# Log-softmax backward: two rows per partition, and all transfers on GpSimd's queue

## The chip, the core and the metric

The kernel runs on one core of a Trainium2 chip. Such a core has engines that work side by side[...]: TensorE (PE, unused here), VectorE (DVE), ScalarE (ACT), GpSimd (POOL) and SyncE (SP). Sixteen transfer engines move data between the large memory of the chip (HBM) and the core's SBUF, a memory of 128 partitions. A transfer (DMA) is issued by an engine's queue, here SP's before and POOL's after, and is split over the sixteen transfer engines. The metric is the device time of one execution in microseconds (us), and less is better. Each kernel is executed several times; one execution is recorded by the profiler.

## What is computed

```python
batch, seq_len, vocab = 8, 1024, 8192          # y and dy: float32

def reference(y, dy):
    softmax_x = np.exp(y)
    sum_dy = np.sum(dy, axis=-1, keepdims=True)
    return (dy - softmax_x * sum_dy).astype(np.float32)
```

There are 8 x 1024 = 8192 rows of 8192 numbers. Each row of dy is summed, and each element of the result takes one exponential, one product and one sum. Two arrays of 268.4 MB are read and one is written, 805.3 MB in all.

## The kernel before

The rows are cut into 64 tiles of 128 rows, one row to each partition, so a tile has 128 x 8192 numbers, 4 MiB, and a partition holds one run of 32 KiB of it.

For each tile, line 65 loads dy into `dy_t`, line 67 loads y into `y_t`, and line 69 lets VectorE sum the row of `dy_t` and put the negative sum in `s_t`. The helper `subtract_scaled_exp` then goes through the tile in four pieces of 2048 columns: ScalarE writes exp(y) to a tile `e_t` in PSUM, a second small memory next to the engines (line 19), and VectorE computes e_t * s_t + dy_t in one scalar_tensor_tensor and writes it over `dy_t` (line 20). Line 75 stores `dy_t`.

Tiles come in batches of three, after a first batch of one. Inside a batch the tiles are loaded and computed one after the other; the stores of the batch stand behind all of them. SP issues all 192 transfers, in the order of the program. An issue that has to wait holds back everything behind it in its queue: a load waits until its buffer is free, and a store until VectorE has finished its tile. The buffers are four `dy_t` (BATCH + 1), two `y_t`, and two `e_t` in PSUM[...]. The order within an engine is the order of the program; semaphores between the engines are put in by the framework.

```python
64            dy_t = dyp.tile([P, D], fp32, name="dy_t")
65            nc.sync.dma_start(out=dy_t[:], in_=dy_f[sl])
66            y_t = yp.tile([P, D], fp32, name="y_t")
67            nc.sync.dma_start(out=y_t[:], in_=y_f[sl])
...
72            subtract_scaled_exp(nc, psum, y_t, dy_t, s_t[:], CD)
73            done.append((sl, dy_t))
74        for sl, dy_t in done:
75            nc.sync.dma_start(out=out_f[sl], in_=dy_t[:])
```

Of the kernel before, what the change touches and what calls it, by code (L numbers as in the profile page):

```python
# [1 line left out]

# [5 lines left out]


ACT_EXP = mybir.ActivationFunctionType.Exp  # L10
ALU = mybir.AluOpType


def subtract_scaled_exp(nc, psum, y_part, dy_part, neg_sum, width):

    total = y_part.shape[-1]
    for c in range(0, total, width):
        e_t = psum.tile([128, width], mybir.dt.float32, name="e_t")
        nc.scalar.activation(e_t[:], y_part[:, c : c + width], ACT_EXP)  # L19
        nc.vector.scalar_tensor_tensor(  # L20
            out=dy_part[:, c : c + width],
            in0=e_t[:],
            scalar=neg_sum,
            in1=dy_part[:, c : c + width],
            op0=ALU.mult,
            op1=ALU.add,
        )


@with_exitstack  # L30
def kernel(
    ctx: ExitStack,
    tc: tile.TileContext,
    y: bass.AP,
    dy: bass.AP,
    out: bass.AP,
):


    nc = tc.nc  # L40
    P = nc.NUM_PARTITIONS
    fp32 = mybir.dt.float32

    y_f = y.flatten_outer_dims()
    dy_f = dy.flatten_outer_dims()
    out_f = out.flatten_outer_dims()
    N, D = y_f.shape
    n_tiles = N // P
    assert N == n_tiles * P
    CD = 2048  # L50
    BATCH = 3

    dyp = ctx.enter_context(tc.tile_pool(name="dyp", bufs=BATCH + 1))
    yp = ctx.enter_context(tc.tile_pool(name="yp", bufs=2))
    psum = ctx.enter_context(tc.tile_pool(name="psum", bufs=2, space=bass.MemoryType.PSUM))
    stats = ctx.enter_context(tc.tile_pool(name="stats", bufs=8))

    first = n_tiles % BATCH
    starts = [0] * bool(first) + list(range(first, n_tiles, BATCH))
    for b, e in zip(starts, starts[1:] + [n_tiles]):  # L60
        done = []
        for i in range(b, e):
            sl = ts(i, P)
            dy_t = dyp.tile([P, D], fp32, name="dy_t")
            nc.sync.dma_start(out=dy_t[:], in_=dy_f[sl])  # L65
            y_t = yp.tile([P, D], fp32, name="y_t")
            nc.sync.dma_start(out=y_t[:], in_=y_f[sl])  # L67
            s_t = stats.tile([P, 1], fp32, name="s_t")
            nc.vector.tensor_reduce(  # L69
                out=s_t[:], in_=dy_t[:], axis=mybir.AxisListType.X, op=ALU.add, negate=True  # L70
            )
            subtract_scaled_exp(nc, psum, y_t, dy_t, s_t[:], CD)
            done.append((sl, dy_t))
        for sl, dy_t in done:
            nc.sync.dma_start(out=out_f[sl], in_=dy_t[:])  # L75


# [1 line left out]
_INS = ['y', 'dy']  # L79
_OUTS = [((8, 1024, 8192), 'float32')]  # L80


# [23 lines left out]
```

## Time and profile before

| | |
|---|---|
| median of 4 runs | 1871.87 us (1871.59 to 1871.94) |
| the profiled execution, its own time | 1871.79 us |
| its span in the profile | 1869.8 us |
| bytes moved in it | 805.38 MB, 431 GB/s on average |
| sum of a row tile (line 69) | 64 times, 8680 ns each |
| exponential of a piece (line 19) | 256 times, 1877 ns each |
| multiply and add of a piece (line 20) | 256 times, 2344 ns each |
| transfers | 64 of dy, 64 of y, 64 of out, 4 MiB each |

The span runs from the first to the last recorded event on the core; the time of an execution is about 2 us longer. Engine rows name an engine, its busy time, its share of the span and its instructions. The rows of 40 digits cut the span into 40 equal slices; a digit is the busy share in tenths, 9 meaning 90% or more, and the row GB/s is what the transfer engines moved in each slice. "L20" is line 20 of the kernel, "SPq" the issuing of transfers by SP. An entry such as "ACT e_t L19 <- DMA y_t<-in_y_dram" says that ScalarE, before it could write e_t, waited for the load of y.

The trace also holds a record of each packet that a transfer engine moved, with its start, length and size, and of the semaphore updates with which transfers report that they have landed.

### The profile page before, as it was taken

The numbers are of one execution on the slowest core, as the hardware profiler recorded it, in microseconds if no ns is written. First come the engines' busy times: TensorE is split into PE (matmuls) and PEld (weight loads), VectorE is DVE, ScalarE is ACT, GpSimd is POOL, SyncE is SP. The second block draws the span as 40 slices with busy tenths as digits, with TensorE's granted clock in tenths as the row PEclk, the third lists the DMA queues.
The fourth block names the chain that finished last, engine by engine and source line by source line (L and its number), as shares of the span: only waits on it lengthen the run. The fifth ranks groups of instructions, "written<-read, shape, count | busy, mean of one in ns | idle before, by whom it ended". The sixth has DMA issues, their size and how long they took to land.

```text
span 1869.8 us, 1067 instructions
## 1 busy us (share of the span) xinstructions
DVE 1136.0 (61%) x320; ACT 477.5 (26%) x257; POOL 0.2 (0%) x4
## 2 busy tenths in 40 slices
DVE  6738384756657383839384655647383839374655
ACT  2214131313223131314131313213131414131322
POOL 0000000000000000000000000000000000000000
DMA  9999999999999999999999999999999999999998
GB/s 404 436 428 437 428 435 434 430 434 430 435 432 433 433 430 435 430 435 432 432 434 431 435 432 433 433 431 434 432 434 434 430 435 430 435 430 434 433 431 386
DMA packets 27656, 805.38 MB, mean 431 GB/s; under 512 B 3072, under 2 KB 3072, under 8 KB 3072
## 3 DMA queue, kind: packets, MB, share of 16 engines
q1 hardware_dynamic: 27648, 805.32, 100.0%
q14 instruction: 8, 0.07, 0.0%
HBM read 536.87 MB, written 268.44 MB: 431 GB/s over the span
## 4 chain that ended last, share of the span: by engine, by line
DMA 61%; DVE 13%; ACT 5%; SPq 1%; issue 0%; DVEq 0%; ACTq 0%
DMA y_t<-in_y_dram 61%; DVE dy_t L20 13%; ACT e_t L19 5%; SPq L65 0%; SPq L75 0%; DVEq L101 0%; ACTq L19 0%; SPq L67 0%
## 5 line engine op out<-in xcount | busy, mean ns | idle before, releaser
L69 DVE TENSOR_REDUCE s_t<-dy_t 128x1 f32<-128x8192 f32 x64 | 555.5, 8680 | 575.5 <-DMA dy_t<-in_dy_dram 575.5
L19 ACT ACTIVATE e_t<-y_t 128x2048 f32<-128x2048 f32 x256 | 476.2, 1877 | 1370.2 <-DMA y_t<-in_y_dram 1295.1
L20 DVE SCALAR_TENSOR_TENSOR dy_t<-e_t,s_t,dy_t 128x2048 f32<-128x2048 f32 x256 | 584.1, 2344 | 139.5 <-ACT e_t L19 139.5
L19 ACT ACT_TABLE_LOAD x1 | 1.3, 1283 | 0.7 <-PEq L90 0.7
L90 POOL MEMSET const-uint8-127<- 128x1 uint8 x1 | 0.1, 102 | 0.0
L90 POOL MEMSET const-bfloat16-1.0<- 128x1 bf16 x1 | 0.1, 101 | 0.0
L90 POOL MEMSET const-float32-0.0<- 128x1 f32 x1 | 0.1, 98 | 0.2 <-issue 0.2
L90 POOL MEMSET const-float32-1.0<- 128x1 f32 x1 | 0.1, 98 | 0.0
## 6 DMA issues: line engine op xcount, KB each, us to landing
dy_t<-in_dy_dram SPq DMA_DIRECT2D x64, 4096.0 KB, 45.4
y_t<-in_y_dram SPq DMA_DIRECT2D x64, 4096.0 KB, 36.4
out_dram<-dy_t SPq DMA_DIRECT2D x64, 4096.0 KB, 27.7
```

What stands on the lines that cost most here:

```text
L19: nc.scalar.activation(e_t[:], y_part[:, c : c + width], ACT_EXP)
L20: nc.vector.scalar_tensor_tensor(out=dy_part[:, c : c + width], in0=e_t[:], scalar=neg_sum, in1=dy_part[:, c : c + width], op0=ALU.mult, o ...
L69: nc.vector.tensor_reduce(out=s_t[:], in_=dy_t[:], axis=mybir.AxisListType.X, op=ALU.add, negate=True)
L90: nc = _bacc.Bacc("TRN2", target_bir_lowering=False, num_devices=1)
```

## The change

The rows are grouped by 256 instead of 128, and each partition holds two neighbouring rows (R = 2). dy is loaded, and out is stored, in transfers of 8 MiB with one run of 64 KiB per partition; y is loaded in two transfers of 4 MiB per group, one for each of the two rows of a partition, in runs of 32 KiB. There are 32 groups. One reduction per group sums both rows.

The exponential is written over `y_t` in SBUF, in pieces of 4096 columns, and PSUM is no longer used. The buffers are two `dy_t` of 64 KiB and two `y_t` of 32 KiB per partition.

The order of the queue is new as well: the load of the next group's dy is issued ahead of the store of this group, and both stand ahead of the next group's y. The store of the last group but one comes after the last loads, and the last store is split in two. All transfers are issued by GpSimd[...], instead of SP. POOL then has this sequence: dy(0), y(0) twice, dy(1), store(0), y(1) twice, dy(2), store(1), and so on; at the end y(31) twice, store(30), store(31) twice.

```diff
-    for c in range(0, total, width):
-        e_t = psum.tile([128, width], mybir.dt.float32, name="e_t")
-        nc.scalar.activation(e_t[:], y_part[:, c : c + width], ACT_EXP)
-        nc.vector.scalar_tensor_tensor(
-            out=dy_part[:, c : c + width],
-            in0=e_t[:],
-            scalar=neg_sum,
-            in1=dy_part[:, c : c + width],
-            op0=ALU.mult,
-            op1=ALU.add,
-        )
...
-    CD = 2048
-    BATCH = 3
+    R = 2
+    G = N // (P * R)
+    CD = D // 2
...
+    dy_v = dy.flatten_outer_dims().rearrange("(g p r) d -> g p (r d)", p=P, r=R)
...
-    dyp = ctx.enter_context(tc.tile_pool(name="dyp", bufs=BATCH + 1))
-    yp = ctx.enter_context(tc.tile_pool(name="yp", bufs=2))
-    psum = ctx.enter_context(tc.tile_pool(name="psum", bufs=2, space=bass.MemoryType.PSUM))
-    stats = ctx.enter_context(tc.tile_pool(name="stats", bufs=8))
+    dyp = ctx.enter_context(tc.tile_pool(name="dyp", bufs=2))
+    yp = ctx.enter_context(tc.tile_pool(name="yp", bufs=R))
+    stats = ctx.enter_context(tc.tile_pool(name="stats", bufs=2))
...
+    def load_dy(g):
+        dy_t = dyp.tile([P, R * D], fp32, name="dy_t")
+        nc.gpsimd.dma_start(out=dy_t[:], in_=dy_v[g])
+        s_t = stats.tile([P, R], fp32, name="s_t")
+        nc.vector.tensor_reduce(
+            out=s_t[:],
+            in_=dy_t[:].rearrange("p (r d) -> p r d", r=R),
+            axis=mybir.AxisListType.X,
+            op=ALU.add,
+            negate=True,
+        )
+        return dy_t, s_t
+
+    def load_y(g):
+        y_ts = []
+        for r in range(R):
+            y_t = yp.tile([P, D], fp32, name="y_t")
+            nc.gpsimd.dma_start(out=y_t[:], in_=y_v[g][:, r * D : (r + 1) * D])
+            y_ts.append(y_t)
+        return y_ts
+
+    def compute(dy_t, s_t, y_ts):
+        for r in range(R):
+            for c in range(0, D, CD):
+                e = y_ts[r][:, c : c + CD]
+                d = dy_t[:, r * D + c : r * D + c + CD]
+                nc.scalar.activation(e, e, EXP)
+                nc.vector.scalar_tensor_tensor(
+                    out=d, in0=e, scalar=s_t[:, r : r + 1], in1=d, op0=ALU.mult, op1=ALU.add
+                )
+
+    def store(g, dy_t, parts=1):
+        w = R * D // parts
+        for k in range(parts):
+            nc.gpsimd.dma_start(
+                out=out_v[g][:, k * w : (k + 1) * w], in_=dy_t[:, k * w : (k + 1) * w]
+            )
+
+    cur = load_dy(0)
+    for g in range(G):
+        if g < G - 1:
+            y_ts = load_y(g)
+            compute(*cur, y_ts)
+            nxt = load_dy(g + 1)
+            if g < G - 2:
+                store(g, cur[0])
+                cur = nxt
+            else:
+                held, cur = cur, nxt
+        else:
+            y_ts = load_y(g)
+            compute(*cur, y_ts)
+            store(g - 1, held[0])
+            store(g, cur[0], parts=R)
```

More of the change, by code (lines that the diff above doesn't have):

```diff
@@ L7 @@
 from concourse.bass import ts
-ACT_EXP = mybir.ActivationFunctionType.Exp
+EXP = mybir.ActivationFunctionType.Exp
 ALU = mybir.AluOpType
-def subtract_scaled_exp(nc, psum, y_part, dy_part, neg_sum, width):
-    total = y_part.shape[-1]
-    for c in range(0, total, width):
-        e_t = psum.tile([128, width], mybir.dt.float32, name="e_t")
-        nc.scalar.activation(e_t[:], y_part[:, c : c + width], ACT_EXP)
-        nc.vector.scalar_tensor_tensor(
-            out=dy_part[:, c : c + width],
-            in0=e_t[:],
-            scalar=neg_sum,
-            in1=dy_part[:, c : c + width],
-            op0=ALU.mult,
-            op1=ALU.add,
-        )
 @with_exitstack
@@ L42 @@
     fp32 = mybir.dt.float32
[L44 to L49, printed above, removed]
-    CD = 2048
-    BATCH = 3
-    dyp = ctx.enter_context(tc.tile_pool(name="dyp", bufs=BATCH + 1))
-    yp = ctx.enter_context(tc.tile_pool(name="yp", bufs=2))
-    psum = ctx.enter_context(tc.tile_pool(name="psum", bufs=2, space=bass.MemoryType.PSUM))
-    stats = ctx.enter_context(tc.tile_pool(name="stats", bufs=8))
@@ L58 @@
[L58 to L65, printed above, removed]
-            y_t = yp.tile([P, D], fp32, name="y_t")
[L67 to L70, printed above, removed]
-            )
[L72 to L75, printed above, removed]
+    N, D = y.flatten_outer_dims().shape
@@ new lines @@
+    R = 2
+    G = N // (P * R)
+    assert N == G * P * R
+    CD = D // 2
+    y_v = y.flatten_outer_dims().rearrange("(g p r) d -> g p (r d)", p=P, r=R)
+    dy_v = dy.flatten_outer_dims().rearrange("(g p r) d -> g p (r d)", p=P, r=R)
+    out_v = out.flatten_outer_dims().rearrange("(g p r) d -> g p (r d)", p=P, r=R)
+    dyp = ctx.enter_context(tc.tile_pool(name="dyp", bufs=2))
+    yp = ctx.enter_context(tc.tile_pool(name="yp", bufs=R))
+    stats = ctx.enter_context(tc.tile_pool(name="stats", bufs=2))
```

## The prediction, made before the changed kernel had run

> **What bounds the kernel now.** I read the page first: engine shares, then the slices.
>
> ```profile
> DVE 1136.0 (61%) x320; ACT 477.5 (26%) x257; POOL 0.2 (0%) x4
> ...
> DMA  9999999999999999999999999999999999999998
> GB/s 404 436 428 437 428 435 434 430 434 430 435 432 433 433 430 435 430 435 432 432 434 431 435 432 433 433 431 434 432 434 434 430 435 430 435 430 434 433 431 386
> DMA packets 27656, 805.38 MB, mean 431 GB/s; under 512 B 3072, under 2 KB 3072, under 8 KB 3072
> ...
> q1 hardware_dynamic: 27648, 805.32, 100.0%
> q14 instruction: 8, 0.07, 0.0%
> ```
>
> No engine computes more than 61% of the span, while the transfer engines are busy in every slice and move 428 to 437 GB/s from the second to the second-last. The chain of waits says "DMA 61%; DVE 13%; ACT 5%", which looks like compute on the path; it is not, since the data movers have queued work under all of it. The waits confirm that the compute engines wait for data:
>
> ```profile
> ACT e_t L19 <- DMA y_t<-in_y_dram: 1295.1, 63, 40.7
> DVE s_t L69 <- DMA dy_t<-in_dy_dram: 575.5, 22, 28.3
> ```
>
> (Columns: total us, times, longest.) Then stages, to see where rate is lost (us, DVE, ACT and POOL busy, clock, DMA share, GB/s):
>
> ```profile
> 0.00:46.00 46.00, 27.30 (x7) 11.54 (x7) 0.20 (x4) 1.00 0.97 405
> 400.00:487.40 87.40, 52.95 (x16) 22.32 (x12) 0.00 (x0) 1.00 1.00 433
> 1827.00:1870.00 43.00, 22.37 (x8) 9.32 (x5) 0.00 (x0) 1.00 0.88 380
> ```
>
> A batch of three tiles (9 transfers of 4 MiB) takes 87.4 us and has no hole. What is left is the rate inside the stream, some 3 us at the head and some 5 us at the tail.
>
> Last I read the trace's packet records. A 32 KiB data packet takes 1213 ns (median), the next starts 3 to 4 ns before its end, and each transfer ends on each of the 16 engines with a 4-byte completion packet of 9 ns. The first engine to complete does so at 1835.32, 1845.00, 1854.68 and 1864.36 us for the last four transfers: 9.684 us each. The last engine completes the first transfer at 12.46 against 12.11 for the first engine, the last transfer at 1868.55 against 1864.36. So the slowest engine falls 3.8 us behind the fastest over the run, and it sets the end. The eight 8 KiB instruction fetches (row q14) come at 271, 359, 438, 930, 1106, 1164, 1542 and 1844 us; completions of one engine each drop back by 0.5 to 1.0 us at most of these. The rest of the drift lies in load packets that take 1218 ns instead of 1213.
>
> [...]
>
> **The change part by part** (own time of the profiled run 1871.79 us: span 1869.8 and 2.0 outside it; median 1871.87, so differences carry over).
>
> *64 KiB runs.* Before: 192 transfers, 1536 data and 192 completion packets per engine. After: dy 32 x 8, y 64 x 8, out 31 x 8 + 2 x 8, that is 1032 data and 129 completion packets. Removed: 504 x 4.65 ns = 2.3 us and 63 x 9 ns = 0.6 us: **-2.9 us** on every engine. If the software generator cuts 64 KiB into two, the first term goes (-0.6 is left). No packet of 64 KiB has been seen; bounds -2.9 to 0.
>
> *Fewer instructions.* ACT goes from 256 activations to 128, DVE from 320 operations to 160, SP's 192 issues become 129 on POOL. About half the instructions, so I estimate 3 or 4 fetches in place of 8. The slowest engine, which took several, then loses one or two: 3.8 us of drift become about 1.5, **-2.3 us**. Bounds: 0 (fetches unchanged) to -3.5.
>
> *Pipeline.* The new queue order is dy(g+1), store(g), y(g+1) twice, dy(g+2), store(g+1). One queue holds everything, so each wait on POOL holds back all behind it. Take 0 as the moment the slowest engine ends the second y half of g. From before: completion to ACT start 0.6 us (1868.55 to landing at 1869.03, plus 0.1). An activation of 4096 is twice the 1.877 us less a fixed part: 3.6 to 3.75. The scalar_tensor_tensor of 4096 is at most 2 x 2.28 = 4.57 (2048 elements took 2344 ns with the wait for the first of each four, 2.28 us apart[...]). So store(g) is free at 0.6 + 3.7 + 2 x 4.5 = 13.3 us; the first half of g has ended before (its y came 9.7 us earlier; its DVE work ends at about 3.5), and the reduction of dy(g), 2 x 8.68 = 17.4 us, earlier still, since dy(g) landed 38 us before. [...] The slowest engine is busy with dy(g+1) until 19.3 us. Slack 4 us, so **0**; each microsecond beyond it would cost 31 us, once per group. The wait of dy(g+2) for store(g)'s landing (about 39 us) holds only store(g+1) behind it, and 8 MiB of y, until 58, lie in the queue. DVE per group is 17.4 + 4 x 4.5 = 35 of 58 us: no bound.
>
> *Exp in place* frees PSUM, which nobody waited for longer than 0.6 us at a time; ACT is idle over 70%: 0.
>
> *Head and tail.* The first packet came 1.0 us after SP's first issue at 0.73. Through GpSimd I estimate 0.7 us more (bounds 0.3 and 2), since nothing covers it. The first transfer has to land in full before compute begins, 8 MiB instead of 4; y and dy(1) are queued behind it, covered. At the end store(30), 19.4 us, covers compute(31), 15 us; the last stores run bare as now. The end on POOL: +0.3 (0 to 2). **+1.0** together.
>
> *Memory pattern.* Engines read 64 KiB apart per partition rather than 32, y in every second 32 KiB; write and read stretches alternate each 58 us instead of 87. The load packets of 1218 ns appear late in a run of six loads and vanish behind stores; runs are now equal to four. I take -0.5 (bounds -1.5 to +5).
>
> Sum: -2.9 - 2.3 + 0 + 1.0 - 0.5 = **-4.7 us**, 1871.87 - 4.7 = **1867.2 us**, 0.25% less. Below 0.2% (3.7 us) counts here as no change.
>
> **Rivals.**
> A, the forecast: gains as summed, 1864 to 1870. [...] Against: three of its terms are only bounded. 48%; about three fifths of it lie under 1868.1.
> B, the software rings also cut the cost that remains[...]: the last 1032 x 4.65 = 4.8 us and part of the drift go too, 1861. Nothing in the trace before speaks for it. 16%.
> C, the change doesn't do what it says: 64 KiB runs are cut, or GpSimd's queue makes one engine drift as instruction fetches did: -0.6 + 1.0 - 0.5, about 1871.5. 13%.
> D, slower: **each descriptor[...] costs the engine more**[...]. 1161 packets per engine; to reach +0.2% (1875.6) from 1867.2 takes 8.4 us, 7.2 ns each[...]. At 15 ns: 1885; the place would be longer spacing between packets on some or all engines[...]. 23%, with late stores (a descriptor writer over 6 us behind DVE's end) as the same cost moved to the issue.
>
> **How the numbers follow.** Likeliest A: 1867.2, its own range 1864 to 1870. Faster: 0.29 of A + 0.16 of B = 0.45. Same: 0.19 of A + 0.12 of C = 0.31. Slower: 0.23 of D + 0.01 of C = 0.24. The range 1859 to 1877 holds A, most of B, C and the mild end of D.
>
> **What would show it.** Packets: 16 512 data and 2 064 completions, 18 576 in all, if 64 KiB stay whole; more shows C. Under 8 q14 packets confirms the second term. Middle slices at 433 to 435 GB/s confirm A; at 435 with spacing below 4 ns, B; under 430, D. POOL's wait for DVE at L77 should end 13 us after y lands, with no slice of DMA under 9; a gap between dy and store would break the pipeline step. A first dy landing beyond 22.5 us would mean the head is mis-sized. The prediction is wrong if steady groups take more than 58.2 us.

## The result and the profile after

The changed kernel took 1875.94 us (median of 38 runs, 1868.89 to 1879.97) against 1871.68 us for the kernel before (58 runs, 1871.30 to 1872.03): ratio 1.002, 95% interval 1.0015 to 1.0025. It is 4.3 us slower, where 4.7 us less was forecast, and it varies by 11 us from run to run where the kernel before varies by 0.7: seven of its 38 runs lie between 1868.9 and 1870.7, the others between 1872.1 and 1880.0. The profiled execution, one of the slower ones, took 1878.48 us, with a span of 1876.7.

From the page of the changed kernel: engine shares, rate per slice, packets, queues.

```profile
DVE 1119.2 (60%) x160; ACT 457.2 (24%) x129; POOL 68.1 (4%) x133
...
GB/s 409 428 427 432 446 426 432 432 431 443 429 428 432 435 427 443 416 432 437 434 427 423 426 446 425 427 430 428 435 426 441 428 425 442 426 429 425 427 434 374
DMA packets 18582, 805.36 MB, mean 429 GB/s; under 512 B 2064, under 2 KB 2064, under 8 KB 2064
...
q0 software_dynamic: 18576, 805.31, 99.8%
q14 instruction: 6, 0.05, 0.0%
```

The 18 576 packets are those that were forecast: runs of 64 KiB stay whole on GpSimd's queue. Six instruction fetches remain, not three or four. The transfer engines are busy in every slice, and yet the mean rate fell from 431 to 429 GB/s.

The waits of the changed kernel (total us, times, longest) show POOL's queue standing where SP's stood:

```profile
ACT y_t L69 <- DMA y_t<-in_y_dram: 1385.9, 64, 42.7
POOL out_dram L77 <- DVE dy_t L70: 1010.2, 32, 55.4
POOL dy_t L45 <- DMA out_dram<-dy_t: 739.0, 30, 26.0
...
DVE s_t L47 <- DMA dy_t<-in_dy_dram: 240.5, 32, 23.6
```

32 of the 33 stores wait for VectorE. The timeline of one group of the changed kernel (start, length, what, and what ended the idle time before) is the view to read closely:

```profile
745.31 7.12 ACT L69 ACTIVATE y_t<-y_t 128x4096 f32<-128x4096 f32 x2 [2.59 <-DMA y_t<-in_y_dram]
748.96 8.88 DVE L70 SCALAR_TENSOR_TENSOR dy_t<-y_t,s_t,dy_t 128x4096 f32<-128x4096 f32 x2 [0.84 <-ACT y_t L69]
758.13 0.54 POOL L77 DMA_DIRECT2D out_dram<-dy_t  x1 [31.49 <-DVE dy_t L70]
758.66 1.05 POOL L60 DMA_DIRECT2D y_t<-in_y_dram  x2
765.05 17.22 DVE L47 TENSOR_REDUCE s_t<-dy_t 128x2 f32<-128x16384 f32 x1 [7.21 <-DMA dy_t<-in_dy_dram]
784.62 0.53 POOL L45 DMA_DIRECT2D dy_t<-in_dy_dram  x1 [24.92 <-DMA out_dram<-dy_t]
```

The slowest engine ends the second half of y at 744.8, ScalarE starts on it at 745.3, and the store is queued 12.8 us later, at 758.1. The two loads of y, behind it in POOL's queue, follow at 758.7, though VectorE had read the first one's buffer to the end at 748.1. VectorE starts to sum the next dy at 765.0. But the engines do not run level: by the completion packets the first engine ends that dy at 759.8, 1.7 us after the store was queued, and the last at 764.7. The packet records carry no engine number, but a packet starts 3 to 4 ns before the packet ahead of it on its engine ends, so that the records can be strung into 16 chains. In these, two engines lose 0.3 and 0.5 us in their dy packets between 758 and 765, just after POOL's issues, and the fourteen others lose 0.3 to 0.6 us in their last packet of the store, near 777. Much the same repeats in nearly every group from the tenth on. The first and the last engine stay 4 to 5 us apart, so both lose alike: a group takes 58.4 us (median of the last engine), over the 58.2 that the prediction had set as the sign of being wrong, and no gap stands between dy and store.

An estimate to measure against in the rest of this text: an engine's **floor** is its packets at the spacing that the changed kernel's trace shows from one start to the next (medians: 1209.4 ns for 32 KiB, 2414.1 for 64 KiB) plus 9 ns per completion packet. It is 1859.4 us before and 1856.4 after. From first packet to last completion, the slowest engine needed 7.4 us over its floor before and 15.6 after.

### The profile page after: what moved, and what is told of

Its sections match the earlier page's. It is cut to its first block, busy times and chain, and to the rows that moved or that the text cites. A ratio compares the mean times of both kernels' runs of the same rounds, so it can differ in the third digit from the quotient of the medians.

```text
span 1876.7 us, 712 instructions
## 1 busy us (share of the span) xinstructions
DVE 1119.2 (60%) x160; ACT 457.2 (24%) x129; POOL 68.1 (4%) x133
## 4 chain that ended last, share of the span: by engine, by line
issue 85%; DMA 8%; POOL 3%; DVE 2%; ACT 0%; POOLq 0%; DVEq 0%; PEldq 0%; ACTq 0%
DMA dy_t<-in_dy_dram 3%; DMA out_dram<-dy_t 3%; DMA y_t<-in_y_dram 2%; POOL y_t L60 2%; DVE s_t L47 1%; DVE dy_t L70 1%; POOL out_dram L77 1%; POOL dy_t L45 1%; ACT y_t L69 0%; POOLq L122 0%; POOLq L60 0%; POOLq L77 0%; DVEq L70 0%; PEldq L122 0%; ACTq L69 0%
## 5 line engine op out<-in xcount | busy, mean ns | idle before, releaser
L70 DVE SCALAR_TENSOR_TENSOR dy_t<-y_t,s_t,dy_t 128x4096 f32<-128x4096 f32 x128 | 568.2, 4482 | 491.6 <-ACT y_t L69 491.4
L69 ACT ACTIVATE y_t<-y_t 128x4096 f32<-128x4096 f32 x128 | 455.9, 3608 | 1385.9 <-DMA y_t<-in_y_dram 1385.9
L47 DVE TENSOR_REDUCE s_t<-dy_t 128x2 f32<-128x16384 f32 x32 | 551.0, 17220 | 240.5 <-DMA dy_t<-in_dy_dram 240.5
L77 POOL DMA_DIRECT2D out_dram<-dy_t x33 | 17.7, 536 | 1010.2 <-DVE dy_t L70 1010.2
L45 POOL DMA_DIRECT2D dy_t<-in_dy_dram x32 | 17.0, 532 | 739.8 <-DMA out_dram<-dy_t 739.0
L60 POOL DMA_DIRECT2D y_t<-in_y_dram x64 | 33.5, 528 | 33.8 <-DVE dy_t L70 31.0
```

The source lines that it names most:

```text
L45: nc.gpsimd.dma_start(out=dy_t[:], in_=dy_v[g])
L47: nc.vector.tensor_reduce(out=s_t[:], in_=dy_t[:].rearrange("p (r d) -> p r d", r=R), axis=mybir.AxisListType.X, op=ALU.add, negate=True,)
L60: nc.gpsimd.dma_start(out=y_t[:], in_=y_v[g][:, r * D : (r + 1) * D])
L69: nc.scalar.activation(e, e, EXP)
L70: nc.vector.scalar_tensor_tensor(out=d, in0=e, scalar=s_t[:, r : r + 1], in1=d, op0=ALU.mult, op1=ALU.add)
L77: nc.gpsimd.dma_start(out=out_v[g][:, k * w : (k + 1) * w], in_=dy_t[:, k * w : (k + 1) * w])
```

## The experiments

**GpSimd's queue or the pattern?** First the issuing engine alone was changed, in both kernels, and the 64 KiB runs were undone on both queues.

e1, the changed kernel on SP (all three issues):

```diff
-        nc.gpsimd.dma_start(out=dy_t[:], in_=dy_v[g])
+        nc.sync.dma_start(out=dy_t[:], in_=dy_v[g])
...
```

> The changed kernel with every transfer issued by SP instead of GpSimd. Ring theory (one engine served from GpSimd's software ring loses about 0.4 us per group of 256 rows, and drags the others): the drift goes, 1866 to 1869 us, run-to-run spread under 1 us, last engine at most 4 us behind the first and no wait at the end of stores. Pattern theory (64 KiB runs, or the new order with its short slack, cost the rate): 1874 to 1878 us as with GpSimd, dy transfers of the last engine still near 19.7 us against 19.32.

Measured: 1868.21 us (20 runs, 1867.33 to 1874.46), ratio to the kernel before 0.9985 (0.9978 to 0.9992). The median is where the ring theory had it; the spread of 7 us, with five runs of twenty above 1871, is what it had excluded.

e2, the kernel before on GpSimd (all three issues):

```diff
-            nc.sync.dma_start(out=dy_t[:], in_=dy_f[sl])
+            nc.gpsimd.dma_start(out=dy_t[:], in_=dy_f[sl])
...
```

> The kernel before with every transfer issued by GpSimd and nothing else changed. Ring theory: one engine drifts more than the 4 us of before, 1875 to 1885 us, with several us between runs. Pattern theory: 1872 to 1874 us, steady.

Measured: 1886.19 us (1884.76 to 1887.24), ratio 1.0075 (1.006 to 1.009). So GpSimd's queue costs 14 us in the old order and 7.7 us in the new one. In e2 line 20 has only one SBUF input (e_t is in PSUM), so the 14 us do not come from a second one; and of the 129 issues of the changed kernel only one falls inside a multiply-add with two.

e3, the changed kernel with two separate 128-row tiles in a group, runs of 32 KiB, and e4, the same on SP:

```diff
-    dy_v = dy.flatten_outer_dims().rearrange("(g p r) d -> g p (r d)", p=P, r=R)
+    dy_v = dy.flatten_outer_dims().rearrange("(g r p) d -> g p r d", p=P, r=R)
...
```

> The changed kernel, on GpSimd, with groups of two 128-row tiles (two separate runs of 32 KiB per partition in place of one of 64 KiB); order, sizes of transfers and buffers as in the changed kernel. Ring theory: no better than the changed kernel, 1877 to 1882 us (the 2.3 us of saved descriptors come back, the drift stays or grows with twice the descriptors). Pattern theory, runs of 64 KiB at fault: 1869 to 1872 us.

> As the one before, issued by SP. Against the changed kernel on SP it prices 64 KiB descriptors alone: 504 data packets per engine more at 4.65 ns, so 2.3 us slower than that kernel (1868 to 1871 us). If 64 KiB runs disturb the memory it is faster than that kernel.

Measured: 1878.37 us on GpSimd (1873.48 to 1882.13), ratio 1.0034 (1.0023 to 1.0045); 1870.79 us on SP (1869.26 to 1875.95), ratio 0.9996 (0.9988 to 1.0005). On SP 64 KiB runs are worth 2.6 us, where 2.3 were expected. On GpSimd the medians differ by 2.4 us, but the runs of both kernels spread over 9 to 11, so that pair alone proves nothing. e3 lies in the range of the ring theory, and yet the two runs together speak against it: with half as many descriptors again, GpSimd's queue costs 7.6 us, as with 64 KiB, and not the 11 or so of a price per descriptor.

**Per transfer, or through the late store?** Next the stores were split, and then dy too.

e5 on SP and e6 on GpSimd, each store in two halves, the first queued when its row is done:

```diff
-                store(g, cur[0])
+                store(g, cur[0], parts=R)
...
```

> The changed kernel on SP with every store split in two halves of 4 MiB, each issued when its row is done, so that the first is queued some 15 us instead of 5 us before the slowest engine needs it, and 11 us instead of 1.5 us before the fastest does. If the late store (short slack) causes what is left of run-to-run spread and of lost time on SP: 1865 to 1867 us, spread under 2 us. If the spread has another cause: 1868 us with the same spread (7 us).

> The same on GpSimd. If GpSimd's cost comes through the late store (the engines wait for each other once a group): nearly all of it goes, 1866 to 1870 us. If each transfer from GpSimd's queue costs some engine 0.06 us wherever it stands (so far 7.7 us over 129 transfers, 14.3 over 192): 161 x 0.06 = 10 us over the run on SP, 1875 to 1878 us.

Measured: 1869.18 us on SP (1868.64 to 1871.05), ratio 0.9986 (0.998 to 0.9993); 1874.23 us on GpSimd (1872.00 to 1876.99), ratio 1.0013 (1.0007 to 1.002). The spread on SP shrinks from 7.1 to 2.4 us, as the late store would have it, but the median does not fall. On GpSimd neither number was met.

e7 on GpSimd and e8 on SP, dy in two halves as well, 192 transfers of 4 MiB:

```diff
-        nc.gpsimd.dma_start(out=dy_t[:], in_=dy_v[g])
+        for r in range(R):
+            nc.gpsimd.dma_start(
+                out=dy_t[:, r * D : (r + 1) * D], in_=dy_v[g][:, r * D : (r + 1) * D]
+            )
```

> On GpSimd, all transfers 4 MiB: dy too in two halves, 192 transfers in all, as in the kernel before. Cost per transfer: 11 to 14 us over the same on SP, 1879 to 1884 us. Cost through the late store: as the run before, 1867 to 1871 us.

> The control on SP with 192 transfers of 4 MiB in runs of 32 KiB, new order. By descriptors alone 2.9 us over the kernel with 64 KiB runs on SP and halved stores: 1868 to 1870 us.

Measured: 1875.87 us on GpSimd (1875.29 to 1877.48), ratio 1.0023 (1.0013 to 1.0032); 1871.22 us on SP (1870.71 to 1872.26), ratio 0.9997 (0.9988 to 1.0005). e7 lies between the ranges of the two theories, e8 1.2 us above its own. The gap is 4.7 us with 192 transfers, against 14.3 in e2 with the same number, so there is no fixed price per transfer. The profiled pair shows where these 4.7 us are: the first packet comes at 2.65 us instead of 1.74, and the span ends 4.7 us after the last completion instead of 1.3. Between the two, the slowest engine is 6.8 us over its floor on GpSimd and 7.0 on SP: inside the stream GpSimd's queue costs nothing here.

**The time of the store alone.** The last four runs change only the width of the compute pieces, and by it when the store is queued, on both queues:

```diff
-    CD = D // 2
+    CD = 2048
```

(8192 in e10 and e11; e11 and e12 on SP.)

> The changed kernel with compute pieces of 2048 columns, so each store is queued about 1.3 us earlier (11.5 us instead of 12.8 after the second y half lands). Theory of the late store (a transfer from GpSimd has to be queued well over 2 us before an engine reaches it, else the engines hold each other up): 1871 to 1874 us, 2 to 4 us better than the changed kernel. If GpSimd's cost has nothing to do with when the store is queued: 1875 to 1877 us.

> Pieces of 8192 columns: the store is queued 3.3 us later (16.1 us after the y half lands, 3.2 us before the slowest engine runs out, and before then for any engine more than 1 us ahead). Late-store theory: 1882 us or more. Otherwise: 1874 to 1878 us.

> The same late store on SP. Late-store theory with a longer lead needed on GpSimd alone: SP pays 0 to 4 us, 1868 to 1872 us, so the gap between the queues grows from 7.7 to 10 us or more. If the lateness costs both queues the same: the gap stays near 7.7.

> The earlier store on SP: 1867 to 1868.5 us, with fewer runs above 1870 than with pieces of 4096 (4 of 20) if the late store makes these; candidate for a kernel faster than both.

Measured: e9 1869.88 us (1869.62 to 1871.63), ratio 0.9991 (0.9984 to 0.9998); e10 1887.95 us (1884.50 to 1891.56), ratio 1.0086 (1.0069 to 1.0103); e11 1880.50 us (1876.16 to 1883.20), ratio 1.0044 (1.0028 to 1.0061); e12 1868.51 us (1867.37 to 1869.50), ratio 0.9983 (0.9976 to 0.999). The late-store theory had the direction of e9 right (the kernel came out 1.1 us below its range) and e10 in its range. It was wrong on e11: SP pays for a late store as well, 12 us. The gap between the queues is 7.4 us there; with four runs of each, which spread over 7 us, it can't be told whether it grows. With pieces of 4096, SP pays nothing in the median (e1 against e12), but five runs of e1 are above 1870 us and none of e12.

The timeline of e9, one group:

```profile
743.22 7.31 ACT L69 ACTIVATE y_t<-y_t 128x2048 f32<-128x2048 f32 x4 [2.41 <-DMA y_t<-in_y_dram]
745.16 9.14 DVE L70 SCALAR_TENSOR_TENSOR dy_t<-y_t,s_t,dy_t 128x2048 f32<-128x2048 f32 x4 [0.58 <-ACT y_t L69]
754.60 0.54 POOL L77 DMA_DIRECT2D out_dram<-dy_t  x1 [30.04 <-DVE dy_t L70]
```

and of e10:

```profile
748.21 7.03 ACT L69 ACTIVATE y_t<-y_t 128x8192 f32<-128x8192 f32 x1 [2.69 <-DMA y_t<-in_y_dram]
755.27 8.75 DVE L70 SCALAR_TENSOR_TENSOR dy_t<-y_t,s_t,dy_t 128x8192 f32<-128x8192 f32 x1 [0.96 <-ACT y_t L69]
764.32 0.54 POOL L77 DMA_DIRECT2D out_dram<-dy_t  x1 [34.76 <-DVE dy_t L70]
```

From landing to store it is 11.4 us in e9 and 16.1 in e10. In e9 the first engine ends its dy at 759.3, 4.7 us after the issue; in e10 at 765.5, 1.1 us after. The stretch from 140 to 1800 us (columns as in the prediction) gives the rate, first of the changed kernel, then of e9, then of e10; the kernel before has 433 there:

```profile
140.00:1800.00 1660.00, 988.35 (x142) 408.97 (x115) 59.38 (x113) 1.00 1.00 431
```
```profile
140.00:1800.00 1660.00, 1011.96 (x261) 423.92 (x232) 59.91 (x114) 1.00 1.00 434
```
```profile
140.00:1800.00 1660.00, 972.24 (x84) 397.46 (x57) 59.40 (x113) 1.00 1.00 428
```

The DMA share is 1.00 in all three: an engine that is held up does not look idle, its packet only lasts longer (by up to 0.8 us in the mean, second table). Put together, over the eight kernels with this order of transfers and whole stores (the lead is the time from the issue of a store to the moment the first engine ends the dy ahead of it, median over the groups from the fourth on; both last columns are of the profiled execution):

| kernel | queue | piece | lead, us | slowest engine over floor, us |
|---|---|---|---|---|
| e10 | GpSimd | 8192 | 1.3 | 25.3 |
| e11 | SP | 8192 | 1.5 | 15.1 |
| changed kernel | GpSimd | 4096 | 1.7 | 15.6 |
| e1 | SP | 4096 | 2.1 | 12.1 |
| e3 (32 KiB runs) | GpSimd | 4096 | 3.1 | 6.6 |
| e4 (32 KiB runs) | SP | 4096 | 3.5 | 6.0 |
| e12 | SP | 2048 | 3.7 | 7.6 |
| e9 | GpSimd | 2048 | 4.6 | 7.0 |

In the executions with 3 us of lead or more the slowest engine stands where it stands in the kernel before (7.4); in the four below 2.2 us it stands 5 to 18 us higher. These are single executions and not medians: that of e1 was among its slower ones, those of e3 and e11 were the fastest of eight and of four. That the lead of a kernel differs between its runs, and the time with it, fits this but was not recorded.

The chains of packets show it group by group. What grows is the last data packet of a store. Its excess over the usual length (2418 ns, or 1213 in e3 and e4), in us, is the mean over the engines and the groups of these eight executions:

| lead in the group, us | GpSimd (groups) | SP (groups) |
|---|---|---|
| under 1 | 0.80 (5) | 0.54 (5) |
| 1 to 1.5 | 0.64 (14) | 0.35 (13) |
| 1.5 to 2 | 0.32 (30) | 0.13 (13) |
| 2 to 3 | 0.02 (16) | 0.02 (26) |
| over 3 | 0.00 (51) | 0.00 (59) |

The loss sets in at about 2 us on both queues, and at the same lead GpSimd loses more. It comes and goes inside one execution: in e11 it is at most 0.05 us in the early groups, whose lead is 2.1 us or more, and 0.3 to 0.6 in the last ten, whose lead is 0.8 to 1.5. Over the run it makes 6.3 us per engine in the changed kernel, 16.7 in e10, 7.1 in e11, 2.5 in e1, and under 0.1 in the other four.

## Why the prediction was wrong

**The step that failed** is the one on the pipeline: "Slack 4 us, so **0**". The times in it were right: VectorE ends 13.0 us after the slowest engine has moved y (13.3 forecast), with activations of 3608 ns, where two of 2048 columns take 3754, and multiply-adds of 4482. The slack was counted on the slowest engine, because that one sets the end, and there it was even larger than forecast: 6.4 us instead of 4. (What the forecast set aside for POOL was the author's estimate; POOL issued 0.3 us behind VectorE's end.) But the same text had found the engines 3.8 us apart, and the first one has that much less: its lead was 1.7 us. I took a wait of the engines that are ahead to cost nothing. It is not so: the slowest engine loses time as well, 10.6 us over the run in the last packets of its dy loads against 1.5 in e9. Moving the store 1.4 us earlier (e9) takes 6.1 us from the changed kernel, 1875.94 to 1869.88, and its spread from 11 to 2 us. The term put at 0 was worth 6.1 us. It took both the late store and GpSimd's queue: with SP alone in GpSimd's place (e1) the median loses nothing, and only its profiled execution, one of the slower ones, shows the loss.

**Fewer instructions, -2.3 us: about 0.** Six fetches were left and not three or four (712 recorded instructions, of 1067 before). Nor did the drift shrink: the slowest engine is 7.0 us (e9) and 7.6 us (e12) over its floor, with eight fetches each, and 6.0 us (e4, an execution 1.1 us under its median) with six, against 7.4 before.

**64 KiB runs, -2.9 us: right.** A 64 KiB packet takes 2418 ns on both queues, two of 32 KiB 2426; e1 against e4 gives -2.6 us, where 2.3 were forecast for the data packets alone. The 4.65 ns per packet in the forecast were the author's estimate; in the changed kernel's trace two spacings of 32 KiB are 2418.9 ns and one of 64 KiB is 2414.1, which makes 4.7. The changed kernel against e3 gives -2.4, which is within the spread of these two.

**Head and tail, +1.0 us: +1.6.** The first packet comes at 2.64 us instead of 1.76 (+0.9, 0.7 forecast), and the span ends 2.05 us after the last completion instead of 1.29 (+0.8, 0.3 forecast). The first dy is complete at 23.2 us, past the 22.5 set as the sign of a mis-sized head; on SP (e1) it is at 22.4.

**Memory pattern, -0.5 us:** not tested apart from the rest. That 64 KiB runs harm nothing is shown by e1 and e4.

With these, -3.0 for the descriptors (-2.4, and the 0.6 forecast for the completions), 0 for the fetches, +1.6 and +6.1 are +4.7 us; +4.3 was measured. Two slips of the prediction change nothing: the terms of C sum to -0.1, which is 1871.8 and not 1871.5, and the multiply-adds of 2048 stand 2.26 us apart, not 2.28.

**The rivals.** The measured time lies within the outer range, at the end kept for D. The sign was D's, but its mechanism was not, so that is luck: a price per descriptor of that size is ruled out by e3 and by e9, where GpSimd's queue costs 1.4 us in all (1869.88 against 1868.51), no more than head and tail (0.9 each in the profiled pair). The spacing between packets did not grow either (in the changed kernel a packet still starts 3 to 4 ns before the end of the one ahead); packets did. B and D supposed more of GpSimd's queue than the trace of before, which has no transfer of it, could show. Two engines do lose time first in the changed kernel, but with an early store the slowest engine is no worse on GpSimd (7.0 us over the floor, e9) than on SP (7.6, e12). D's side remark on late stores named the right place and set the threshold at 6 us behind VectorE's end; POOL issues 0.3 us behind it, and that is already too late when the first engine has under 2 us left. The part of C that lets one engine drift under GpSimd comes nearest to what the records show, but the drift follows the late store, not the queue: e9 keeps it at 2.8 us through the middle of the run.

**What stays open.** What in the transfer engines loses the time is not shown. Most engines' loss appears in the last packet of the store, 19 us after its issue, and the slowest's in its last dy packets. A plain gap before a store appears nowhere in the changed kernel; e10 has 36 of 0.1 to 0.6 us. Why GpSimd loses more at the same lead is not shown either; its first packet comes 1.4 us after its first issue and SP's 1.0 us after, which may leave less of the lead. In e6, whose first half store comes early, GpSimd still costs 5.1 us: head and tail explain 0.9 + 2.2 = 3.1, the other 2 us are not located (the profiled pair, 2.9 us apart, loses nothing inside the stream). Of the 14 us of e2, 0.9 lie in the head and 3.3 in the tail. Inside the stream the third store of a batch has 2.5 us of lead (median; 5.3 in the kernel before), and its last packet carries 3.2 us per engine over the run. But the packets of the third y of a batch carry 8 us, and the store behind them was queued 22 us early: in the old order GpSimd's queue has a cost that the late store does not explain.

A kernel faster than both is e12: the change on SP with pieces of 2048, 1868.51 us, ratio 0.9983 (0.9976 to 0.999). e1 has the same median, but not its steadiness.

## What to carry to other kernels

When the transfer engines are the bound, count the slack of a late transfer on the engine that runs ahead, not on the one that sets the end. Here 3 us before the first engine runs out were enough on both queues, and under 2 us were not. A DMA share of 1.00 does not prove that nothing waits (e10 has it at 428 GB/s, the kernel before at 433); compare the packet lengths, or the rate of a long stretch, with the floor. Change the issuing engine by itself before crediting it: here GpSimd's queue only added cost, 1.4 us (e9) to 14 us (e2).

## What the runs showed of the hardware

- The 16 engines end 4.2 us apart after 1.9 ms even in the steady kernel before, and 3.7 to 5.0 us in the changed kernel, e1 and e9. The instruction fetches of 8 KiB run on the same engines, and each of the eight in the kernel before sets one engine back by 0.5 to 1.0 us: the fetch itself takes 0.31 us, and the data packet beside it 0.23 to 0.66 more than 1213 ns.
- A store queued less than 2 us before the first engine runs out of work shows as a longer last packet of that store, by 0.1 to 0.8 us (means of the table), and the DMA share stays at 1.00 (140 to 1800 us, changed kernel and e10). Before a store the changed kernel has no plain gap; e10 has 36, of 0.1 to 0.6 us.
- A kernel that issues through GpSimd ends later after its last completion packet, and by how much varies: 2.0 us (changed kernel), 3.4 (e6), 3.5 (e3), 4.6 and 4.7 (e2 and e7), against 1.1 to 1.3 on SP.
- POOL's issue of a transfer takes 0.53 us. In e2, 21 of 192 issues fall inside a multiply-add with one SBUF input and take as long; with two inputs (line 70) only one issue of the changed kernel does, at 0.54.
- One packet of 64 KiB in place of two of 32 KiB saves 4.7 ns in the changed kernel (2414.1 against 2418.9 from start to start). The lengths, 2418 and 1213 ns, are the same on both queues.
